# Where a chunked scan's matmuls are asked for: products with the inverse moved up to the chunk's first group, key and query products asked for in pairs

## The chip, the core and the metric

The kernel runs on one core of one Trainium2 chip. The metric is device time in microseconds (us) for one execution of the program; three executions were timed, and one more was taken with the hardware profiler. An execution holds one layer of an encoder for a sequence of 1024 tokens and 16 meta tokens, width 1024, everything in 32-bit floats.

## The reference, cut to what matters

The layer normalises its input, projects it with one wide matrix, and splits the result into streams. The stream that the change touches is the gated delta rule, for 8 heads of width 128, once forward and once backward over the sequence. Cut to what matters here, the reference does this for every head and direction:

```python
kk = jnp.einsum("bnhid,bnhjd->bnhij", k, k)                  # keys with keys, inside a chunk
lmat = jnp.where(strict, beta[..., :, None] * kk * decay, 0.0)
a = lmat + jnp.eye(CHUNK)
sol = lax.linalg.triangular_solve(a, rhs, lower=True, unit_diagonal=True)
qk = jnp.einsum("bnhid,bnhjd->bnhij", q, k) * decay          # queries with keys
...
def step(S, inp):                                            # one chunk
    v_new = u_c - jnp.einsum("bhcd,bhde->bhce", w_c, S)
    o_c = (jnp.einsum("bhcd,bhde->bhce", qd_c, S)
           + jnp.einsum("bhij,bhje->bhie", qk_c, v_new))
    S = S * gl_c[..., None, None] + jnp.einsum("bhcd,bhce->bhde", kd_c, v_new)
    return S, o_c
```

Around it stand a short convolution branch, gates, an output projection, a SwiGLU and a final normalisation. The change does not touch those.

## The kernel before, in words

The program has a first stage (the input projection with all eight heads' scans woven into it), and after it stages of large products alone. The change lies in the first stage.

**Dense work.** `dense_steps` (L328) makes the projection: a unit of 128 output columns takes three blocks of tokens (336, 320 and 384 wide, or two of 512), and each block is 24 matmuls into one PSUM bank: eight slices of the width times three terms (high part by high part, high by low, low by high), which together stand in for a full-precision product. The trace names them by their tiles, pm<-hTh,wh, pm<-al,wh and pm<-hTh,wl. There are 3744 of these matmuls in the stage.

**Streams.** Beside the dense units, generators bring the heads along: `g_decay` (masks of decay), `g_norm` (norms, and the products of keys with keys and queries), `g_inv` (the inverse of the triangular matrix), `g_scan` (the walk over chunks). They hand over at every `yield` with the time at which they want to go on. `run_streams` is called between any two dense matmuls and lets each stream that is due issue its next instructions; `pump` does the same for queues of VectorE work (convolutions, the inverse's substitution steps, norms).

**The planner's clock.** Nothing of this is known at run time: the order on each engine is written down once, by a planner that keeps an account T of how far TensorE ("pe"), VectorE ("dve") and ScalarE ("act") have got. `pe(ns)` adds to TensorE's account and returns its end plus 200 ns; `V(n, 1)` adds 130 + 1.042 n ns to VectorE's (263 ns for n = 128) and returns its end plus 370 ns. On the chip each engine then runs its own list in order and waits on semaphores, so where the account is wrong an engine waits, and everything behind the waiting instruction waits with it.

**A chunk of the scan** (`g_scan`, loop over i = 0..7). A head has 8 chunks of 128 tokens, and step i works on chunk i forward and chunk 7 - i backward, so most instructions come in twos. In order: keys by state into bank b1 (L853); queries by state into bank b2 (L856); VectorE makes r0 from b1 (L863); the inner products kept back from the chunk before, PQ by v2 (`late`, L892); the additions to the output (L834 and L839 on VectorE, squares at L843 on ScalarE); the inverse by r0 (L871, tiles pd<-r,NP), which is the step that the change moves; ScalarE scales its result to w and v2 (L878, L883); kn by w (L888); VectorE updates the state S (L902). In the first step of a head one direction has no state yet, so L853, L856 and L863 come once. At a head's end small VectorE instructions make a root (L920 to L499), eight instructions scale the output (L928), TensorE transposes it (L98) and ScalarE copies it out (L943).

**Keys by keys and queries** (`kkq`, L590, in `g_norm`). One matmul per chunk makes both products, 256 columns wide, into a bank of the three banks named pe. VectorE takes them off (L626 twice, L629 once) and the bank is free again; `freed_at` holds when, by the account. `ask` issues the next product once the bank it needs is free by that account.

**The border.** The last unit of dense work in this stage is a gate z; its VectorE step is L465 (tile rb) and its store is L467 (z_d<-rb). Behind it stands the next stage's first work: its own z products (L134 to L136), splits of weights (L179, wl<-raw,wh), and sums of the activations (L179, b<-hTh) in the space that rb used.

## Time and profile before

| | us |
|---|---|
| median of three timed runs | 1973.54 |
| lowest and highest of them | 1972.09, 1974.93 |
| the profiled execution's own time | 1973.36 |
| its span, first to last instruction | 1971.6 |

The profile page gives busy time by engine, a strip of 40 slices, and groups of instructions by source line. Its timeline gives the start and length of each instruction; rows that follow each other on one line are merged, with a count. A 32-bit product shows as two matmul records, so a pair of products reads x4. Lengths of matmuls overlap, since they are pipelined; what a matmul costs TensorE is read from start to start. PE is TensorE, PEld its weight loads, DVE VectorE, ACT ScalarE.

### The profile page before, as it was taken

To read this page: it belongs to the slowest core of one execution; us is meant where nothing else is said; L and a number is where in the kernel's file an instruction comes from. 1 tells how busy PE (TensorE), PEld (TensorE's weight loads), DVE (VectorE), ACT (ScalarE), POOL (GpSimd) and SP (SyncE) were. 2 spreads that over 40 slices of the span, in tenths; PEclk is the share of its full clock that TensorE was granted. 3 is DMA by queue.
4 is the path that set the end of the run, shared out by engine and by line. 5 is a ranking of instruction groups with operands and counts; after the bars stand their busy time and mean duration, and the time that the engine had idled before them with its cause. 6 is when DMAs were issued, how large, how long until landed. Compare 5 with 4: busy or idle time off the path is not lost.

```text
span 1971.6 us, 31923 instructions
## 1 busy us (share of the span) xinstructions
PE 1957.3 (99%) x11992; PEld 1719.6 (87%) x11992; DVE 1398.0 (71%) x3017; ACT 837.7 (42%) x1968; POOL 108.4 (5%) x410
## 2 busy tenths in 40 slices
PE   9999999999999999999999999999999999999998
PEld 8999999999999999888888888888888888878887
DVE  7888688888888888845954544468676765746575
ACT  6462364646464646343444211235333333324344
POOL 2011101010101010100000000000000000000000
PEclk9999999999999999999999999999999999999999
DMA  4122121212121212223246642133366654577654
GB/s 145 61 86 81 55 87 60 77 59 77 59 84 52 87 49 87 65 81 108 85 150 242 245 153 86 65 107 112 103 234 246 245 189 153 178 274 242 193 173 168
DMA packets 124704, 251.53 MB, mean 128 GB/s; under 512 B 44988, under 2 KB 46453, under 8 KB 122117
## 3 DMA queue, kind: packets, MB, share of 16 engines
q1 hardware_dynamic: 123957, 248.44, 37.8%
q8 instruction: 94, 1.54, 0.3%
q10 hardware_dynamic: 592, 1.05, 0.1%
q14 instruction: 61, 0.50, 0.1%
HBM read 181.20 MB, written 68.25 MB: 127 GB/s over the span
## 4 chain that ended last, share of the span: by engine, by line
PE 45%; DMA 3%; DVE 2%; ACT 1%; issue 0%; SPq 0%; DVEq 0%; ACTq 0%
PE pd L1446 12%; PE pe L1446 6%; PE pm L1446 4%; PE pe L2057 1%; PE pe L2055 1%; PE pe L2056 1%; PE pd L2057 1%; PE pd L2055 1%; PE pd L2056 1%; PE pe L134 1%; PE pe L135 1%; PE pd L135 1%; PE pd L134 1%; PE pe L136 1%; PE pd L136 1%; PE pm L2056 1%
## 5 line engine op out<-in xcount | busy, mean ns | idle before, releaser
L328 PE MATMUL pm<-hTh,wh 128*128 128x320 f32 (+4 forms) x1248 | 426.9, 347 | 0.3 <-ACT hTh L1096 0.2
L328 PE MATMUL pm<-hTh,wl 128*128 128x320 f32 (+4 forms) x1248 | 426.8, 347 | 0.0
L328 PE MATMUL pm<-al,wh 128*128 128x320 f32 (+4 forms) x1248 | 423.8, 345 | 0.0
L328 PEld LDWEIGHTS pm<-hTh,wh 128*128 128x128 f32 x1248 | 233.9, 188 | 10.7 <-ACT hTh L1096 0.9
L328 PEld LDWEIGHTS pm<-al,wh 128*128 128x128 f32 x1248 | 233.8, 188 | 10.7
L328 PEld LDWEIGHTS pm<-hTh,wl 128*128 128x128 f32 x1248 | 233.9, 188 | 10.2 <-POOL wl L1111 0.3
L102 DVE TENSOR_TENSOR al<-raw,ring_h 128x1024 fp32r<-128x1024 f32 x73 | 88.6, 1222 | 65.6 <-ACT ring_h L101 64.7
L101 ACT CAST ring_h<-raw 128x1024 fp32r<-128x1024 f32 x73 | 76.6, 1053 | 109.1 <-PE pe L2057 35.0
L982 DVE TENSOR_TENSOR wl<-raw,wh 128x512 fp32r<-128x512 f32 x112 | 75.3, 687 | 34.5 <-ACT wh L985 34.2
L350 DVE SCALAR_TENSOR_TENSOR kq<-ra,wc,kq 128x520 f32<-128x520 f32 x128 | 96.5, 754 | 3.5 <-ACT kq L380 2.0
L878 ACT ACTIVATE w<-pd,small 128x128 f32<-128x128 f32 x128 | 39.8, 362 | 123.4 <-PE pd L871 122.9
L483 DVE TENSOR_TENSOR tm<-fP,fN 128x135 f32<-128x135 f32 (+23 forms) x248 | 72.2, 291 | 4.8
L487 DVE TENSOR_TENSOR fP<-fP,tm 128x135 f32<-128x135 f32 (+23 forms) x248 | 71.9, 290 | 5.0
L985 ACT CAST wh<-raw 128x512 fp32r<-128x512 f32 x112 | 66.3, 624 | 3.8 <-issue 3.6
L101 ACT CAST wh<-raw 128x1024 fp32r<-128x1024 f32 x37 | 38.8, 1047 | 47.8 <-PE pe L135 10.4
L1994 ACT ACTIVATE b<-b 128x512 f32<-128x512 f32 x20 | 12.6, 632 | 101.6 <-DVE b L1412 101.6
L843 ACT ACTIVATE jk<-NP 128x128 f32<-128x128 f32 x64 | 19.9, 311 | 81.1 <-DVE NP L839 80.1
L102 DVE TENSOR_TENSOR wl<-raw,wh 128x1024 fp32r<-128x1024 f32 x37 | 45.1, 1219 | 10.2 <-ACT wh L101 10.0
L1446 PE MATMUL pd<-b_hl,wh 128*128 128x512 f32 x168 | 51.9, 390 | 0.0
L1412 DVE TENSOR_TENSOR b<-pd,b 128x512 f32<-128x512 f32 x21 | 14.5, 689 | 52.5 <-PE pd L1446 47.5
L350 DVE SCALAR_TENSOR_TENSOR vT<-ra,wc,vT 128x520 f32<-128x520 f32 x64 | 48.3, 754 | 1.4 <-ACT vT L380 0.7
L679 POOL TENSOR_TENSOR tm<-mP,mN 1x15 f32<-1x15 f32 (+7 forms) x120 | 36.9, 307 | 210.8 <-DMA mN<-ndm 202.4
(630 smaller groups left out, 4772.1 us busy)
## 6 DMA issues: line engine op xcount, KB each, us to landing
raw<-in_w_in_dram SPq DMA_DIRECT2D x72, 512.0 KB
raw<-in_w_gate_up_dram SPq DMA_DIRECT2D x44, 512.0 KB
sums<-in_w_down_dram SPq DMA_DIRECT2D x22, 512.0 KB
t_d<-sums SPq DMA_DIRECT2D x11, 1024.0 KB
raw<-s_d SPq DMA_DIRECT2D x44, 256.0 KB
raw<-t_d SPq DMA_DIRECT2D x44, 256.0 KB
act_d<-b SPq DMA_DIRECT2D x43, 256.0 KB
raw<-act_d SPq DMA_DIRECT2D x33, 256.0 KB
```

The lines of the kernel that those rows point to most:

```text
L101: nc.scalar.copy(hi, src)
L102: nc.vector.tensor_tensor(out=lo, in0=src, in1=hi.bitcast(F32), op=ALU.subtract)
L134: mm(po[:m, :n], wh[:, k, :m], xhk[:, t0:t0 + n], start=(k == 0), stop=False)
L328: mm(po[:, :n], ww[:, k], f(k)[:, t0:t0 + n], start=i == 0, stop=i == 3 * KT - 1)
L350: nc.vector.scalar_tensor_tensor(out=acc, in0=raw[:, h0 + t:h0 + t + hn], scalar=wc[:, t, col:col + 1], in1=acc, op0=ALU.mult, op1=ALU.add)
L483: nc.vector.tensor_tensor(out=tv, in0=fP[:, 0:r, j:j + 1].broadcast_to([P, r, n]), in1=fN[:, j:j + 1, j + 1:32].broadcast_to([P, r, n]), o ...
L487: nc.vector.tensor_tensor(out=fP[:, 0:r, j + 1:32], in0=fP[:, 0:r, j + 1:32], in1=tv, op=ALU.subtract)
L878: nc.scalar.activation(w[d], b2[:, 2 + d], AF.Copy, scale=ce[:, c, d:d + 1])
L982: nc.vector.tensor_tensor(out=u[1][1][:, k], in0=u[2][:, k], in1=u[1][0][:, k].bitcast(F32), op=ALU.subtract)
L985: nc.scalar.copy(u[1][0][:, k], u[2][:, k])
L1446: mm(po, x[:, k], at(y, k), start=i == 0 and not add_to, stop=i == 11, skip_group_check=add_to)
L2056: mm(bank[t], h_[:, c], l_[:, hi], start=False, stop=False)
```

## The change

In `ask`, the products of keys with keys and queries are issued two at a time, once the bank that the second of them needs is free by the account. In `g_scan`, the planner now counts VectorE's r0 as started at the end of the first pair (L853) and not of the second; the products of queries by state are written behind r0's instructions (they are L863 in the new file, and r0 is L859), and the products with the inverse (still L871) follow at once in the same group, without handing over, wherever by the account r0 will be there within 150 ns. Elsewhere the stream hands over as before.

```diff
--- before.py
+++ after.py
@@ -596,9 +596,9 @@
         def ask():
 
             nonlocal asked
-            while asked < NC and asked < len(freed_at) + 2 and freed_at[asked - 2] <= T["pe"]:
-                nxt.append(kkq(asked))
-                asked += 1
+            while asked < NC and asked - 1 < len(freed_at) and freed_at[asked - 1] <= T["pe"]:
+                nxt.extend((kkq(asked), kkq(asked + 1)))
+                asked += 2
         yield T["act"] + HOP
         nc.vector.tensor_scalar(out=ssk1, in0=ssk, scalar1=EPS, scalar2=None, op0=ALU.add)
         nc.vector.reciprocal(rk2, ssk1)
@@ -851,11 +851,7 @@
             b1, b2 = newbank(), newbank()
             for d in act_:
                 mm(b1[:, d], kT[:, cs(cd[d])], S[d], start=True, stop=True)
-            t = pe(215 * len(act_))
-            for d in act_:
-                mm(b2[:, d], qT[:, cs(cd[d])], S[d], start=True, stop=True)
             pe(215 * len(act_))
-            yield t
             r0 = [vS[:, cd[0]], vS[:, cd[1]]]
             for d in act_:
                 c = cd[d]
@@ -863,10 +859,14 @@
                 nc.vector.scalar_tensor_tensor(out=r0[d], in0=b1[:, d], scalar=negEG[:, c, hd[d]:hd[d] + 1], in1=vS[:, c],
                                                op0=ALU.mult, op1=ALU.add)
                 t = V(P, 1)
+            for d in act_:
+                mm(b2[:, d], qT[:, cs(cd[d])], S[d], start=True, stop=True)
+            pe(215 * len(act_))
             while late:
                 late.pop(0)()
             outputs()
-            yield t
+            if t > T["pe"] + 150:
+                yield t
             for d in range(2):
                 mm(b2[:, 2 + d], NP[:, cd[d], d], r0[d], start=True, stop=True)
             yield pe(430)
```

TensorE, early in the stage, head 0: the third and the fourth product of keys (L590) before, among dense matmuls (L328).

```order
L590 MATMUL pe_1489<-kq_308 128x256
L328 MATMUL pm_1452<-hTh,wh_1284 128x336
L328 MATMUL pm_1452<-al_126,wh_1284 128x336
L328 MATMUL pm_1452<-hTh,wl_1285 128x336
L328 MATMUL pm_1452<-hTh,wh_1284 128x336
L328 MATMUL pm_1452<-al_126,wh_1284 128x336
L328 MATMUL pm_1452<-hTh,wl_1285 128x336
L328 MATMUL pm_1510<-hTh,wh_1284 128x320
L328 MATMUL pm_1510<-al_124,wh_1284 128x320
L328 MATMUL pm_1510<-hTh,wl_1285 128x320
L590 MATMUL pe_1517<-kq_308 128x256
L328 MATMUL pm_1510<-hTh,wh_1284 128x320
```

The same place now:

```order
L328 MATMUL pm_1506<-al_124,wh_1284 128x320
L328 MATMUL pm_1506<-hTh,wl_1285 128x320
L590 MATMUL pe_1515<-kq_308 128x256
L590 MATMUL pe_1517<-kq_308 128x256
L328 MATMUL pm_1506<-hTh,wh_1284 128x320
L328 MATMUL pm_1506<-al_124,wh_1284 128x320
```

The third product no longer goes out ahead by itself; it waits for the fourth one's bank and both stand together.

TensorE, the last chunk of the last head, before: first pair, second pair, kept inner products, three dense matmuls, then the products with the inverse.

```order
L853 MATMUL pd_11993<-S_11979,kq_9477 128x128
L853 MATMUL pd_11993<-S_11981,kq_9477 128x128
L856 MATMUL pd_11994<-S_11979,kq_9477 128x128
L856 MATMUL pd_11994<-S_11981,kq_9477 128x128
L892 MATMUL pd_11932<-v_2028_11963,PQ_10011 128x128
L892 MATMUL pd_11932<-v_2029_11965,PQ_10011 128x128
L328 MATMUL pm_11974<-al_124,wh_11796 128x512
L328 MATMUL pm_11974<-hTh,wl_11797 128x512
L328 MATMUL pm_11974<-hTh,wh_11796 128x512
L871 MATMUL pd_11994<-r_2036_11999,NP_10480 128x128
L871 MATMUL pd_11994<-r_2037_12001,NP_10480 128x128
L328 MATMUL pm_11974<-al_125,wh_11796 128x512
```

And now:

```order
L853 MATMUL pd_12016<-S_12006,kq_9399 128x128
L853 MATMUL pd_12016<-S_12008,kq_9399 128x128
L863 MATMUL pd_12017<-S_12006,kq_9399 128x128
L863 MATMUL pd_12017<-S_12008,kq_9399 128x128
L892 MATMUL pd_11968<-v_2030_11992,PQ_10074 128x128
L892 MATMUL pd_11968<-v_2031_11994,PQ_10074 128x128
L871 MATMUL pd_12017<-r_2038_12020,NP_10323 128x128
L871 MATMUL pd_12017<-r_2039_12022,NP_10323 128x128
L328 MATMUL pm_12001<-hTh,wh_11701 128x512
```

The three dense matmuls that stood between the inner products and the inverse's are gone to other places; eight products of the scan stand in a row. In the whole program 18 of the 64 chunks are ordered like this (one of them with a dense matmul ahead of each L871); in the other 46 L871 still stands apart. The number of times that dense work is broken into falls from 358 to 331.

VectorE at the border, before: the root's last steps, the scaling of the output (L928), with the last two steps of gates z (L465) around it.

```order
L498 SCALAR_TENSOR_TENSOR small_10144<-small_10144 128x9
L499 SCALAR_TENSOR_TENSOR small_10144<-small_10144 128x9
L928 TENSOR_SCALAR NP_10480<-NP_10480,small_10144 128x128
L465 SCALAR_TENSOR_TENSOR rb_12045<-rb_12045,pm_11974 128x512
L928 TENSOR_SCALAR NP_10480<-NP_10480,small_10144 128x128 x7
L179 TENSOR_TENSOR wl_12148<-raw_12129,wh_12147 128x1024
L465 SCALAR_TENSOR_TENSOR rb_12095<-rb_12095,pm_12047 128x512
L179 TENSOR_TENSOR b_2054_12125<-hTh 128x2048
```

And now:

```order
L498 SCALAR_TENSOR_TENSOR small_10063<-small_10063 128x9
L179 TENSOR_TENSOR wl_12148<-raw_12129,wh_12147 128x1024
L465 SCALAR_TENSOR_TENSOR rb_12083<-rb_12083,pm_12001 128x512
L499 SCALAR_TENSOR_TENSOR small_10063<-small_10063 128x9
L497 TENSOR_TENSOR small_10063<-small_10063 128x9
L498 SCALAR_TENSOR_TENSOR small_10063<-small_10063 128x9
L499 SCALAR_TENSOR_TENSOR small_10063<-small_10063 128x9
L928 TENSOR_SCALAR NP_10323<-NP_10323,small_10063 128x128 x8
L179 TENSOR_TENSOR b_2054_12125<-hTh 128x2048
```

The last L465, whose store the next stage's L179 on b waits for, now stands ahead of the root's last four steps and of L928, and behind its first steps; L928 has become the last thing of the stage.

TensorE at the border, before: the last dense matmuls, then the eight transposes of the last head's output.

```order
L328 MATMUL pm_12047<-al_126,wh_11796 128x512
L328 MATMUL pm_12047<-hTh,wl_11797 128x512
L328 MATMUL pm_12047<-hTh,wh_11796 128x512
L328 MATMUL pm_12047<-al_126,wh_11796 128x512
L328 MATMUL pm_12047<-hTh,wl_11797 128x512
L98 MATMUL pd_12099<-ident,NP_10480 128x128 x4
L98 MATMUL pd_12106<-ident,NP_10480 128x128 x4
```

And now, 17 matmuls of the next stage's z (L134 to L136) later:

```order
L135 MATMUL pe_12150<-al_125,wh_12143 128x512
L136 MATMUL pe_12150<-hTh,wl_12144 128x512
L134 MATMUL pe_12150<-hTh,wh_12143 128x512
L98 MATMUL pd_12099<-ident,NP_10323 128x128 x3
L135 MATMUL pe_12150<-al_126,wh_12143 128x512
L98 MATMUL pd_12099<-ident,NP_10323 128x128
L98 MATMUL pd_12106<-ident,NP_10323 128x128 x2
L136 MATMUL pe_12150<-hTh,wl_12144 128x512
L98 MATMUL pd_12106<-ident,NP_10323 128x128 x2
L134 MATMUL pe_12150<-hTh,wh_12143 128x512
```

The transposes now stand among the next stage's products.

## Prediction, made before the changed kernel ran

> **What bounds the kernel now.** I read the page first, then who TensorE waited for, then the stretches of the first stage.
>
> ```profile
> span 1971.6 us, 31923 instructions
> PE 1957.3 (99%) x11992; PEld 1719.6 (87%) x11992; DVE 1398.0 (71%) x3017; ACT 837.7 (42%) x1968; POOL 108.4 (5%) x410
> ```
>
> ```profile
> PE pd L98 <- POOL ident masks.py:199: 1.5, 1, 1.5
> PE pe L1446 <- ACT b L1989: 1.2, 1, 1.2
> PE pe L590 <- DVE PQ L629: 1.1, 2, 0.8
> PE pe L98 <- DVE xr L1082: 0.9, 1, 0.9
> PE pm L2056 <- DVE al L102: 0.8, 1, 0.8
> PE pd L98 <- DVE ss L162: 0.7, 1, 0.7
> PE pm L328 <- ACT hTh L1096: 0.2, 1, 0.2
> ```
>
> ```profile
> 300.00:500.00 200.00, 200.00 (x1711) 192.26 (x1710) 172.29 (x505) 103.67 (x343) 23.84 (x94) 1.00 0.23 70
> 500.00:700.00 200.00, 200.00 (x1707) 191.54 (x1706) 173.72 (x519) 104.81 (x347) 23.26 (x94) 1.00 0.23 68
> 700.00:923.00 223.00, 222.85 (x1753) 201.07 (x1752) 159.00 (x497) 102.98 (x331) 21.28 (x79) 1.00 0.23 73
> ```
>
> The first numbers behind each stretch are its length and TensorE's busy time; they are equal, with the granted clock at 1.00. In the whole span TensorE waited 1.5 + 1.2 + 1.1 + 0.9 + 0.8 + 0.7 + 0.2 = 6.4 us for others, and of these the change can reach one row: L590 behind L629, 1.1 us in two places. So TensorE bounds the stage, and what counts is what its matmuls cost from start to start and whether it newly waits. That the scan's chain becomes shorter is worth nothing by itself.
>
> A row of busy time does not prove that the array has no room. [...]
>
> **The change part by part.** First, what does a group cost? The last chunk of the last head:
>
> ```profile
> 911.42 0.40 PE L328 MATMUL pm<-hTh,wh 128*128 128x512 f32 x1
> 911.66 0.61 PE L853 MATMUL pd<-S,kq 128*128 128x128 f32 x4
> 912.10 0.61 PE L856 MATMUL pd<-S,kq 128*128 128x128 f32 x4
> 912.31 0.61 DVE L863 SCALAR_TENSOR_TENSOR r<-pd,negEG,vS 128x128 f32<-128x128 f32 x2 [0.47 <-PE pd L853]
> 912.55 0.61 PE L892 MATMUL pd<-v,PQ 128*128 128x128 f32 x4
> 912.92 0.48 PE L328 MATMUL pm<-al,wh 128*128 128x512 f32 x1
> 913.24 0.39 PE L328 MATMUL pm<-hTh,wl 128*128 128x512 f32 x1
> 913.46 0.40 PE L328 MATMUL pm<-hTh,wh 128*128 128x512 f32 x1
> 913.70 0.61 PE L871 MATMUL pd<-r,NP 128*128 128x128 f32 x4
> 914.06 0.47 PE L328 MATMUL pm<-al,wh 128*128 128x512 f32 x1
> 914.37 0.39 PE L328 MATMUL pm<-hTh,wl 128*128 128x512 f32 x1
> ```
>
> A dense matmul of 512 takes 0.23 us to the next start (913.24 to 913.46, 913.46 to 913.70 a little more). The one right behind a group takes 0.31 or 0.32, which looks like a fee of 0.08 for each group. But it is the tail of the last small product: the group of six takes 913.24 - 911.66 - 0.23 = 1.35 us, or 0.225 a product, and the group of two takes 914.37 - 913.70 - 0.23 = 0.44, or 0.22 a product. Twos, fours and sixes cost the same for each product. Eight in a row come to 8 x 0.222 = 1.78 against 1.35 + 0.44 = 1.79: **0.01 us for each of the 18 chunks, 0.2 us in all**.
>
> The same for the keys, one product and then two:
>
> ```profile
> 124.83 0.59 PE L590 MATMUL pe<-kq 128*128 128x256 f32 x2
> 125.07 0.53 PE L328 MATMUL pm<-hTh,wh 128*128 128x384 f32 x1
> 125.44 0.33 PE L328 MATMUL pm<-al,wh 128*128 128x384 f32 x1
> 125.61 0.33 PE L328 MATMUL pm<-hTh,wl 128*128 128x384 f32 x1
> 142.84 1.03 PE L590 MATMUL pe<-kq 128*128 128x256 f32 x4
> 143.51 0.59 PE L328 MATMUL pm<-hTh,wl 128*128 128x512 f32 x1
> 143.94 0.40 PE L328 MATMUL pm<-hTh,wh 128*128 128x512 f32 x1
> ```
>
> One costs 125.44 - 124.83 - 0.17 (a dense matmul of 384) = 0.44 us, two cost 143.94 - 142.84 - 0.23 = 0.87. Two singles are 0.88. With 64 such products the pairs save 0.01 x 32 or 0.3 us at the very most; I count 0.1. What the pairs can take away is the wait for L629: between 0 and the 1.1 us of its row. The first of a pair now uses a bank that has been free for longer, and the second comes 0.435 us behind it (half of 0.87), which is cover for a bank that VectorE frees a little late. I take 0.6 off, near the middle since neither end has a better row.
>
> Next, what the 18 new places of L871 can cost. Nothing dense stands between L892 and L871 any more, so if r0 is late, TensorE stands still and all dense work stands behind it. In the rows above, VectorE was free: r0 began 0.65 us after L853 began (912.31 - 911.66) and both were done 0.61 later, at 1.26. In a row of eight, the first L871 has its turn at 6 x 0.222 = 1.33 and needs the first r0, and the second at 1.55 and needs the second: it is there 0.3 us early. Where VectorE is busy it looks like this:
>
> ```profile
> 418.60 0.74 PE L853 MATMUL pd<-S,kq 128*128 128x128 f32 x4
> 419.80 0.60 DVE L863 SCALAR_TENSOR_TENSOR r<-pd,negEG,vS 128x128 f32<-128x128 f32 x2
> ```
>
> Here r0 began at 1.20 and ended at 1.80, which would hold the second L871 up by 1.80 - 1.55 = 0.25 us. The bounds are thus 0 and 18 x 0.25 = 4.5 us. The change chooses its places by the planner's account: t is VectorE's start plus 2 x 263 + 370 = 896 ns, and TensorE stands at 2 x 430 = 860 ns past the end of the first pair, so t is under 860 + 150 only where VectorE is at most 114 ns behind at that end. That picks the cases of the first kind. I take 0.2 us for all 18, for a few in which the account is off, and keep 4.5 as the far end.
>
> In the other 46 chunks L871 is asked for up to 0.43 us sooner than before. In the rows above it came at 913.70, 0.78 us after r0's end at 912.92, so this uses up slack and adds no wait; cost 0, or the same 0.25 each where the account is badly off. ScalarE's steps behind L871 and the S update behind them keep their distance to it.
>
> Last, the border. What is moved there is VectorE's list, and with it the store of the last gate:
>
> ```profile
> 916.46 0.60 PE L892 MATMUL pd<-v,PQ 128*128 128x128 f32 x4
> 921.40 0.29 DVE L928 TENSOR_SCALAR NP<-NP,small 128x128 f32<-128x128 f32 x1
> 922.21 1.46 DVE L928 TENSOR_SCALAR NP<-NP,small 128x128 f32<-128x128 f32 x7
> 923.05 1.04 PE L98 MATMUL pd<-ident,NP 128*128 128x128 f32 x8
> 924.10 1.22 DVE L179 TENSOR_TENSOR wl<-raw,wh 128x1024 fp32r<-128x1024 f32 x1 [0.44 <-ACT wh L1497]
> 925.24 0.68 DVE L465 SCALAR_TENSOR_TENSOR rb<-rb,pm 128x512 f32<-128x512 f32 x1
> 931.15 2.29 DVE L179 TENSOR_TENSOR b<-hTh 128x2048 f32<-128x2048 f32 x1 [5.23 <-DMA z_d<-rb]
> ```
>
> Before, 27 dense matmuls stood between the last inner products and the end of the dense work at 923.05; now 10 do, so L892 is at about 923.05 - 10 x 0.23 - 0.45 = 920.3. L928 began 921.40 - 916.46 = 4.94 us after it. Now L179 and L465 also stand ahead of it, from 924.10 to 925.24 and on to 925.92 less 0.08 of overlap, 1.7 us: L928 begins at about 920.3 + 4.94 + 1.7 = 926.9 and its eight end near 928.7 (1.46 us for seven makes 0.21 each). TensorE comes to the first L98 after 17 matmuls of the next stage, at 923.05 + 17 x 0.23 = 927.0, and would be through eight transposes and the two matmuls between them by 928.3; its last one waits until about 928.8. That is a new wait of **0.7 us** (0 to 1.5, as the estimate of L928 shifts). Behind it, VectorE's long sums (L179 on b) do not start when VectorE is free, but when the store of the last gate has landed, 5.23 us after VectorE had stopped. L465 moves by about 0.2 to 0.4 us, so these sums do too; I count that as covered by TensorE's own 0.7.
>
> The sum against the profiled execution: -0.2 - 0.1 - 0.6 + 0.2 + 0.7 = 0.0 us on its 1973.36 us (span 1971.6 and 1.76 around it). The median of the runs is 0.18 above it, so the forecast for a median is **1973.5 us**.
>
> **The rivals.** *A group does have a fee.* Then the 0.08 us behind each group is real and 27 fewer groups (358 to 331) save 27 x 0.08 = 2.2 us: 1971.3. For it speaks the row of 0.31 behind each group, against it the equal cost of a product in twos and sixes. Chance 0.10. [...]
>
> *VectorE is late where the planner believes it free.* L871 in its new place then holds up TensorE, the engine that bounds the stage: 18 x 0.25 = 4.5 us, 1978. It decides where r0's second half ends later than 1.55 us after L853's start. For it: the row at 419.80. Against it: VectorE's account is kept op by op, and at 912.31 VectorE sat idle for 0.47 us waiting for L853. Chance 0.07.
>
> *The border passes its delay on.* If the last L465 slips by the whole tail of the root and not by 0.4, the sums on b, and what TensorE takes from them, slip too; I price it at the eight L928, from 926.9 to 928.7: another 1.8 us, 1975.3. Against it stands the order: L465 is ahead of L928. Chance 0.12.
>
> **How the numbers follow.** Forecast 0.69, fee 0.10, late VectorE 0.07, border 0.12, and 0.02 for something that gives TensorE more than all of its visible waits. A measurement of this kernel can tell about 0.2%, 3.9 us, from no change. The forecast, the fee and the border are within it: 0.91. Late VectorE is the slower side, 0.07; faster is 0.02. The range goes from the fee's 1971.3, a little lower for the run-to-run spread of the times before, to past the border's 1975.3: 1971.0 to 1976.2. It leaves out late VectorE and the far ends, about 1 in 10.
>
> **What would show each step.** In the new profile, eight products in a row at 1.78 us and pairs of L590 at 0.87 confirm that there is no fee; rows of eight shorter than 1.7 refute it. A row of waits with L871 behind L859 shows late VectorE, with its sum. The row of L590 behind L629 should be gone or under 0.5 us. A wait of L98 behind L928 near 927 us, and the start of L179 on b near 931.4, test the border. The prediction is wrong if TensorE's waits in the first stage differ from before by more than some 2 us.

## The result, and the profile after

The changed kernel takes 1987.57 us (median of six runs, 1983.48 to 1991.55) against 1974.94 us for the kernel before on the same chip (six runs, 1972.09 to 1976.74). The ratio is 1.0064 with a 95% interval of 1.005 to 1.0079: it is **12.6 us slower**. I had forecast no difference, 1973.5 us.

The two profiled executions lie 15.1 us apart (1988.45 and 1973.36 us). The page after, its span and its busy time by engine:

```profile
span 1986.7 us, 31921 instructions
PE 1964.1 (99%) x11992; PEld 1720.2 (87%) x11992; DVE 1398.1 (70%) x3017; ACT 838.4 (42%) x1968; POOL 109.5 (6%) x410
```

The counts of each engine's instructions are the same as before. The last dense matmul (L328) of the first stage starts at 937.15 us where it started at 922.82, so 14.3 of the 15.1 us arise in that stage. Whom TensorE waited for in the kernel after (total us, number of times, longest):

```profile
PE pd L853 <- DVE S L902: 2.3, 6, 0.7
PE pe L590 <- DVE PQ L629: 1.9, 2, 1.4
PE pd L1446 <- DVE b L1412: 1.9, 1, 1.9
PE pd L738 <- issue: 1.8, 1, 1.8
PE pe L98 <- DVE xr L1082: 1.8, 1, 1.8
PE pd L98 <- POOL ident masks.py:199: 1.5, 1, 1.5
PE pm L328 <- DVE wl L982: 0.9, 1, 0.9
...
PE pd L98 <- DVE NP L928: 0.6, 2, 0.4
...
PE pd L759 <- DVE XT L751: 0.4, 1, 0.4
PE pd L806 <- DVE wide L804: 0.3, 1, 0.3
```

The row of L871, where I looked for a late VectorE, is not there. New in the stage are the rows of L853, L738, L328 behind L982, L928, L759 and L806, and L590 has grown from 1.1 us. Each is small, and they lie in different places. The grown row of L98 behind L1082 (0.9 us before) lies ahead of the stage's first dense matmul, which starts at the same time as before (13.47 us, 13.51 before); the new row of L1446 behind L1412 lies behind the stage, at 1517.30 us.

This list knows only idle time that the profiler could name. I therefore sorted the stage in a second way, from the start of its first dense matmul to the start of its last. Each TensorE instruction takes the time from its predecessor's start to its own; from it goes the median that the same neighbourhood (line and width of the predecessor and of the one before, line of the instruction) has in the nineteen kernels of the table below, and the rest is put down to the instruction that came late. "At the scan" below sums this for the products of a chunk (L853, L856, L871, L888, L892 by their text), "elsewhere" is all other lines. Kernels are to be compared, the absolute value means little. For the kernel before it gives 0.3 us at the scan and 5.8 elsewhere, for the changed one 6.2 and 14.1: **+5.9 at the scan, +8.3 elsewhere**. The medians themselves sum to 0.2 us more. Together 14.4 us, the stage's whole loss.

**The scan's share.** One of the six places, in the changed kernel's timeline (start, length, engine, operation, idle time before it in brackets):

```profile
723.58 0.60 PE L888 MATMUL pd<-w,kn 128*128 128x128 f32 x4
...
723.72 1.17 ACT L985 CAST wh<-raw 128x512 fp32r<-128x512 f32 x2
...
724.40 0.69 DVE L982 TENSOR_TENSOR wl<-raw,wh 128x512 fp32r<-128x512 f32 x1 [1.88 <-ACT wh L985]
...
726.32 0.59 DVE L902 SCALAR_TENSOR_TENSOR S<-S,eGl,pd 128x128 f32<-128x128 f32 x2
...
726.71 0.75 PE L853 MATMUL pd<-S,kq 128*128 128x128 f32 x4 [0.73 <-DVE S L902]
```

The chunk was done early on TensorE (L888 at 723.58). But VectorE stood for 1.88 us at a step of a weight split (L982) whose cast (L985) ScalarE only began at 723.72, and four small steps followed that (725.01 to 726.32) before the state's update L902 had its turn. TensorE then came to the next chunk's L853 0.73 us too early. In the other five places VectorE idles less, or not at all; L902 simply stands behind its queue (steps L350, L358, L483, L487, L982). The chunk ahead of the wait shown is one of the 18 with a row of eight; in four of the six places it is one in which L871 stands apart.

**Elsewhere.** Three stalls make up the most of it. First, a readback: the inverse's data go out by the stores L689, come back by the loads L694, and VectorE takes them at L713. The last head's, before and after:

```profile
840.19 1.66 SPq L689 DMA_DIRECT2D pd<-fP  x3
...
849.11 1.93 SPq L694 DMA_DIRECT2D NP<-pd  x4
...
851.56 0.43 DVE L713 STREAM_TRANSPOSE XT<-NP 32x256 f32<-32x256 f32 x1 [2.49 <-DMA NP<-pd]
```

```profile
862.45 1.66 SPq L689 DMA_DIRECT2D pd<-fP  x3
...
870.57 3.31 SPq L694 DMA_DIRECT2D NP<-pd  x4
...
876.23 0.43 DVE L713 STREAM_TRANSPOSE XT<-NP 32x256 f32<-32x256 f32 x1 [10.55 <-DMA NP<-pd]
...
880.10 1.29 DVE L982 TENSOR_TENSOR wl<-raw,wh 128x512 fp32r<-128x512 f32 x2
...
880.85 0.50 PE L328 MATMUL pm<-hTh,wl 128*128 128x512 f32 x1 [0.89 <-DVE wl L982]
```

The way from L689 to L713 took 11.4 us before (851.56 - 840.19) and 13.8 after. But VectorE now reached L713 when only some 3 us of it had gone by, at 876.23 - 10.55 = 865.7, since in the new list less of its work stands ahead of it; it stood for 10.55 us where it had stood for 2.49. The weight split L982 is queued behind it, and TensorE waits 0.89 us for that. A smaller case, 2.95 us, comes shortly before the longest wait of L590, at the second product of a pair:

```profile
692.97 0.43 DVE L713 STREAM_TRANSPOSE XT<-NP 32x256 f32<-32x256 f32 x1 [2.95 <-DMA NP<-pd]
...
695.03 0.42 DVE L629 TENSOR_TENSOR PQ<-pe,PQ 128x256 f32<-128x256 f32 x1
...
695.61 0.67 PE L590 MATMUL pe<-kq 128*128 128x256 f32 x2 [1.40 <-DVE PQ L629]
```

Second, TensorE stopped in a burst of 32 by 32 products, 1.80 us for which the profile names no engine ("issue"), and third, its granted clock was 0.50 right behind that:

```profile
592.61 0.24 PE L738 MATMUL pd<-NP,T 32*32 32x32 f32 x4
594.65 0.18 PE L738 MATMUL pd<-NP,T 32*32 32x32 f32 x1 [1.80 <-issue]
...
597.81 0.63 PE L328 MATMUL pm<-hTh,wh 128*128 128x512 f32 x1
598.24 0.63 PE L328 MATMUL pm<-al,wh 128*128 128x512 f32 x1
```

Dense matmuls of 512 columns are 0.43 us apart there, where 0.23 is usual. The stretch of the stop and the one behind it (length, TensorE's busy time, granted clock):

```profile
592.00:595.90 3.90, 2.10 (x102) 1.00 0.06 19
595.92:599.31 3.39, 3.39 (x10) 0.50 0.02 5
```

At half clock for 3.4 us, TensorE loses an estimated 1.7 us (0.50 x 3.4). The stop costs 1.8 us and the wait for L982 0.9; with the L590 row's growth of 0.8 these are 5.2 of the 8.3 us elsewhere. The rest is scattered in pieces of some tenths.

### The profile page after: what moved, and what is told of

It reads as the page before. It is cut to its first block, busy times and chain, and to the rows that moved or that the text cites. A ratio compares the mean times of both kernels' runs of the same rounds, so it can differ in the third digit from the quotient of the medians.

```text
span 1986.7 us, 31921 instructions
## 1 busy us (share of the span) xinstructions
PE 1964.1 (99%) x11992; PEld 1720.2 (87%) x11992; DVE 1398.1 (70%) x3017; ACT 838.4 (42%) x1968; POOL 109.5 (6%) x410
## 3 DMA queue, kind: packets, MB, share of 16 engines
q8 instruction: 94, 1.54, 0.3%
## 4 chain that ended last, share of the span: by engine, by line
PE 52%; DMA 3%; DVE 2%; issue 0%; SPq 0%; ACT 0%; DVEq 0%; ACTq 0%
PE pd L1446 13%; PE pe L1446 6%; PE pm L1446 4%; PE pm L328 2%; PE pe L135 1%; PE pe L134 1%; PE pe L136 1%; PE pe L2056 1%; PE pe L2055 1%; PE pe L2057 1%; PE pd L2056 1%; PE pd L2055 1%; PE pd L2057 1%; PE pd L134 1%; PE pd L135 1%; PE pd L136 1%
## 5 line engine op out<-in xcount | busy, mean ns | idle before, releaser
L328 PE MATMUL pm<-al,wh 128*128 128x320 f32 (+4 forms) x1248 | 426.1, 347 | 0.0
L328 PE MATMUL pm<-hTh,wh 128*128 128x320 f32 (+4 forms) x1248 | 424.9, 346 | 0.3 <-ACT hTh L1096 0.2
L328 PE MATMUL pm<-hTh,wl 128*128 128x320 f32 (+4 forms) x1248 | 423.9, 345 | 0.9 <-DVE wl L982 0.9
L328 PEld LDWEIGHTS pm<-hTh,wl 128*128 128x128 f32 x1248 | 234.1, 189 | 11.7 <-DVE wl L982 1.3
L328 PEld LDWEIGHTS pm<-hTh,wh 128*128 128x128 f32 x1248 | 234.1, 189 | 11.3 <-ACT hTh L1096 0.9
L328 PEld LDWEIGHTS pm<-al,wh 128*128 128x128 f32 x1248 | 234.1, 189 | 10.3
L982 DVE TENSOR_TENSOR wl<-raw,wh 128x512 fp32r<-128x512 f32 x112 | 76.5, 689 | 33.4 <-ACT wh L985 33.0
L350 DVE SCALAR_TENSOR_TENSOR kq<-ra,wc,kq 128x520 f32<-128x520 f32 x128 | 96.9, 757 | 1.2 <-DVE kq L350 0.5
L483 DVE TENSOR_TENSOR tm<-fP,fN 128x135 f32<-128x135 f32 (+23 forms) x248 | 72.5, 292 | 4.5 <-DMA fN<-nd 1.0
L487 DVE TENSOR_TENSOR fP<-fP,tm 128x135 f32<-128x135 f32 (+23 forms) x248 | 72.1, 291 | 4.8
L985 ACT CAST wh<-raw 128x512 fp32r<-128x512 f32 x112 | 66.8, 627 | 3.7 <-issue 3.6
L1994 ACT ACTIVATE b<-b 128x512 f32<-128x512 f32 x20 | 12.6, 631 | 104.8 <-DVE b L1412 104.8
L1412 DVE TENSOR_TENSOR b<-pd,b 128x512 f32<-128x512 f32 x21 | 14.5, 689 | 53.8 <-PE pd L1446 53.8
L533 ACT ACTIVATE PQ<-PQ,negG 128x128 f32<-128x128 f32 x128 | 43.1, 394 | 21.3 <-DVE PQ L528 21.2
L1446 PE MATMUL pd<-b_hl,wh 128*128 128x512 f32 x168 | 51.9, 390 | 0.0
L350 DVE SCALAR_TENSOR_TENSOR vT<-ra,wc,vT 128x520 f32<-128x520 f32 x64 | 48.4, 756 | 2.5 <-ACT vT L380 1.3
```

Of the source, the lines that this page charges most:

```text
L328: mm(po[:, :n], ww[:, k], f(k)[:, t0:t0 + n], start=i == 0, stop=i == 3 * KT - 1)
L350: nc.vector.scalar_tensor_tensor(out=acc, in0=raw[:, h0 + t:h0 + t + hn], scalar=wc[:, t, col:col + 1], in1=acc, op0=ALU.mult, op1=ALU.add)
L483: nc.vector.tensor_tensor(out=tv, in0=fP[:, 0:r, j:j + 1].broadcast_to([P, r, n]), in1=fN[:, j:j + 1, j + 1:32].broadcast_to([P, r, n]), o ...
L487: nc.vector.tensor_tensor(out=fP[:, 0:r, j + 1:32], in0=fP[:, 0:r, j + 1:32], in1=tv, op=ALU.subtract)
L533: nc.scalar.activation(PQ[:, c, d], PQ[:, c, d], AF.Exp, bias=negG2[:, c, hd:hd + 1])
L982: nc.vector.tensor_tensor(out=u[1][1][:, k], in0=u[2][:, k], in1=u[1][0][:, k].bitcast(F32), op=ALU.subtract)
```

## The experiments

My theory when I began (A) was that the change's visible parts are right in the forecast, but that a re-ordered plan meets waits that the planner's account does not hold, wherever they are. The rivals: the early booking of r0 makes the state's updates late (B); TensorE is held at L871 (C, the one priced in the prediction); the pairs of keys cost it (D). The account's entries that the edits change are: ARRIVE, the delay in ns after which a mask's load is taken to be there, and LAND, that after which a store is taken to have landed, so that its data can be read back; `pe(435)`, the booking of one product L590.

### All runs

Each line is against the kernel before on the same chip: difference of medians, ratio's 95% interval, chunks in rows of eight, then the two sums of the second sorting for the profiled execution, which is one execution of each kernel.

| kernel | us | against before | 95% interval | rows of eight | at the scan | elsewhere |
|---|---|---|---|---|---|---|
| before | | 0 | | 0 | 0.3 | 5.8 |
| e15_replan_arrive2 | 1973.93 | -0.3 | 0.9991 to 1.0009 | 0 | 1.1 | 4.9 |
| e8_replan_land | 1974.45 | +0.2 | 0.9991 to 1.001 | 0 | 0.7 | 7.6 |
| e4_replan_arrive | 1976.93 | +3.4 | 1.0005 to 1.0024 | 0 | 1.9 | 6.2 |
| e16_replan_land2 | 1978.49 | +4.3 | 1.0015 to 1.0034 | 0 | 1.7 | 11.2 |
| e7_replan_kkq | 1979.3 | +5.0 | 1.0015 to 1.0034 | 0 | 0.7 | 11.7 |
| e1_keys_alone | 1979.39 | +5.9 | 1.0018 to 1.0037 | 0 | 0.7 | 10.6 |
| e3_scan_no_merge | 1977.0 | +3.5 | 1.0004 to 1.0024 | 0 | 2.9 | 6.7 |
| e18_scan_slack | 1976.9 | +3.5 | 1.0007 to 1.0026 | 0 | 2.4 | 7.3 |
| e11_after_no_merge | 1979.33 | +6.1 | 1.0021 to 1.0047 | 0 | 4.1 | 7.0 |
| e2_scan_alone | 1980.63 | +7.1 | 1.0022 to 1.0046 | 17 | 7.0 | 7.2 |
| e9_after_land | 1979.06 | +5.8 | 1.0023 to 1.0044 | 16 | 5.7 | 7.5 |
| e10_after_kkq | 1980.9 | +7.6 | 1.0025 to 1.0055 | 16 | 4.2 | 8.3 |
| the change | 1987.57 | +12.6 | 1.005 to 1.0079 | 18 | 6.2 | 14.1 |
| e12_scan_booked | 1979.58 | +6.3 | 1.0022 to 1.0048 | 30 | 4.2 | 9.3 |
| e5_after_booked | 1980.42 | +6.2 | 1.0015 to 1.0041 | 35 | 4.7 | 10.2 |
| e13_booked_land | 1981.45 | +7.3 | 1.0023 to 1.0053 | 38 | 7.8 | 6.6 |
| e14_booked_kkq | 1983.74 | +9.6 | 1.0031 to 1.0064 | 37 | 7.1 | 7.8 |
| e17_after_gap | 1980.05 | +6.7 | 1.0019 to 1.0046 | 19 | 2.8 | 10.3 |

(e6_after_split, +55.4 us, is left out here; it loses in another way, told below.)

### The two parts apart

e1_keys_alone is the kernel before with the pairs of keys:

```diff
-            while asked < NC and asked < len(freed_at) + 2 and freed_at[asked - 2] <= T["pe"]:
-                nxt.append(kkq(asked))
-                asked += 1
+            while asked < NC and asked - 1 < len(freed_at) and freed_at[asked - 1] <= T["pe"]:
+                nxt.extend((kkq(asked), kkq(asked + 1)))
+                asked += 2
```

> The kernel before with only the key and query products asked for in twos. If the loss of 12.6 us lies in holding TensorE at the inverse's products (theory C) or in booking VectorE's r0 too early (theory B), this one is within 1 us of before. If any re-ordering of the plan costs, because waits arise between engines that the planner's account does not hold (theory A), it is 2 to 10 us slower than before. If the pairs themselves are at fault (theory D), it carries most of the 12.6 us and its waits stand at L590.

e2_scan_alone is the kernel before with the rest of the change; e3_scan_no_merge is that with the hand-over always made:

```diff
-            if t > T["pe"] + 150:
-                yield t
+            yield t
```

> The kernel before with only the change to the scan (r0 booked from the end of the first pair, 17 merged groups). Theories B and C: 10 to 13 us slower than before. Theory A: some 2 to 12 us slower, and not the rest of what the keys alone leave. Theory D: within 1 us of before.

> The scan's change with the early booking of r0, but the stream always hands over before the inverse's products, so that none stands in the first group. Theory C: within 1 us of before. Theory B: 8 to 13 us slower, as the booking is the same. Theory A: slower by some 2 to 12 us, with waits in other places than in the changed kernel.

Measured: +5.9 us for the keys, +7.1 for the scan's part, +3.5 for it without merging. The first two add up to 13.0, about the whole. In e2 the seventeen rows of eight take 1.782 to 1.796 us, median 1.79, so merging holds nobody up in the row itself: theory C falls for this kernel, and for the change, whose merged rows lose 0.15 us at L871 by the second sorting. (In the four kernels below that merge 30 to 38 chunks, they lose 0.9 to 2.2 us there.) The groups of six that are left take 1.475 us in the mean in e2 and 1.450 in the change, where all take 1.353 before: 39 x 0.12 = 4.8 us, nearly all of it waiting for S. The keys' loss is another thing. TensorE's waits in e1, the first row:

```profile
PE pd L98 <- DVE NP L746: 2.3, 1, 2.3
```

One wait of transposes for a step of an inverse, which ends at 286.31 us and is no product of keys; the row of L590 has gone from the list.

### What any new plan costs

Five kernels have nothing changed but one figure of the planner's account, so that it writes the same program in another order: e4_replan_arrive, e7_replan_kkq, e8_replan_land, and later e15_replan_arrive2 and e16_replan_land2.

```diff
-    ARRIVE = 10000
+    ARRIVE = 10400
```

```diff
-            return pk, pe(435)
+            return pk, pe(445)
```

```diff
-    LAND = 5500
+    LAND = 5700
```

```diff
-    ARRIVE = 10000
+    ARRIVE = 9600
```

```diff
-    LAND = 5500
+    LAND = 5300
```

> The kernel before, with none of the change: one constant of the planner's account (how long a mask's load takes to arrive) is 10400 ns in place of 10000. The same instructions on each engine, in an order that differs in a hundred places on TensorE. Theory A: 2 to 10 us slower than before. Theories B, C and D: within 1.5 us of before.

> The kernel before with none of the change: a product of keys is booked at 445 ns in place of 435, the smallest shift of the plan that was tried (about a third as many rows stand elsewhere as in the other re-plan). Theory A: 0 to 6 us slower than before. Theories B, C and D: within 1.5 us of before.

> The kernel before with none of the change: a store's landing is booked at 5700 ns in place of 5500. Theory A: 1 to 8 us slower than before. Theories B, C and D: within 1.5 us of before.

> The kernel before with ARRIVE at 9600 ns where 10000 stood; nothing else. Scatter of plans: +0 to +5 us, as the three neutral plans so far (+3.4, +5.0, +0.2), by waits in other places. If the plan of the kernel before is in no way singled out, there should be plans below it as well: -3 to +3 us.

> The kernel before with LAND at 5300 ns where 5500 stood; nothing else. Scatter of plans: +0 to +5 us. If the plan of the kernel before is not singled out: -3 to +3 us.

Measured: +3.4, +5.0, +0.2, -0.3 and +4.3 us. Theory A is shown as far as it goes: a plan alone moves the time by up to 5 us. The dearest of them has the keys' wait as its first row:

```profile
PE pd L98 <- DVE NP L746: 2.5, 1, 2.5
```

e16 has it too (2.3 us). So e1's +5.9 lies hardly above what neutral plans give, by the same wait, and theory D has no run that bears it out. The kernel before is at the low end of its six plans, whose mean is 2.1 us above it.

Is the change's 12.6 us then such an accident as well? e9_after_land and e10_after_kkq are neutral plans of the changed kernel:

```diff
-    LAND = 5500
+    LAND = 5700
```

```diff
-            return pk, pe(435)
+            return pk, pe(445)
```

> The whole change, with the planner's LAND at 5700 ns where 5500 stood; nothing else. This only makes another plan of the changed kernel. Theory A (most of the loss comes with the plan that happened to come out, since each plan meets other waits): the loss moves by several us, to anywhere from +4 to +16 us against the kernel before. Rival (the loss belongs to the change itself, above all to the early booking of r0): it stays at +11 to +14.5 us.

> The whole change, with a product of keys with keys and queries booked at 445 ns where 435 stood; nothing else. A second neutral plan of the changed kernel. Theory A: +4 to +16 us, and not where the first one is. Rival (a property of the change): +11 to +14.5 us, as the changed kernel itself.

Measured: +5.8 and +7.6 us. About half of the 12.6 us is an accident of the one plan: "elsewhere" falls from 14.1 to 7.5 and 8.3 us, which is within what plans of the kernel before have (4.9 to 11.7). But "at the scan" stays, 5.7 and 4.2 us. By their medians all three plans of the changed kernel lie above all six plans of the kernel before, though the nearest two, e9 at +5.8 and e7 at +5.0 us, overlap in their intervals. At the scan the two sets are clear of each other: 4.2 to 6.2 against 0.3 to 1.9 us. Theory A alone does not carry that.

### Booking r0 where it starts

Theory B says that the account takes r0 to start with the end of the pair, while in the rows it starts later. In the quoted row of the prediction r0 began 0.65 us after L853 began, which is 0.215 after the pair's 0.43. e5_after_booked books that, with the bound for merging moved by the same amount; e12_scan_booked does so without the keys; e13_booked_land and e14_booked_kkq are e5 with the two neutral edits of e9 and e10.

```diff
             r0 = [vS[:, cd[0]], vS[:, cd[1]]]
+            T["dve"] = max(T["dve"], T["pe"] + 215)
...
-            if t > T["pe"] + 150:
+            if t > T["pe"] + 365:
```

> The changed kernel, but VectorE's r0 is booked from 215 ns behind the end of the first pair, which is where the trace of before shows it to start (0.645 us behind the first start, not 0.43), and the bound for merging is raised by the same 215 ns; 35 chunks merge in place of 18. Theory B (the early booking makes the account run ahead of VectorE): most of the loss of 12.6 us goes, to under 4 us slower than before. Theory A (any re-ordered plan meets waits that the account does not hold): still 3 to 12 us slower than before, with waits at other places. If merging itself held TensorE up (theory C), it would be slower than the changed kernel by 5 us or more.

> The scan's part alone, with r0 booked where VectorE really begins it, 215 ns behind the end of the pair, and merged by the same rule. Theory B (the early booking makes the S updates late): the waits of L853 behind S are gone, the groups that are not merged go back to some 1.39 us, and the time is +0 to +4 us against the kernel before, where the scan's part with the early booking was +7.1. Rival (the order of writing, queries by state behind r0, costs by itself): +6 to +8 us still.

> The changed kernel with r0 booked right, and LAND at 5700 ns. If what was left (+6.2 us) is the scatter of plans, this plan lands somewhere else, in the spread that plans of the kernel before have: 0 to +5 us, with no row of L853 behind S over 0.5 us. If it is a property of the change, +5.5 to +7 us again.

> The changed kernel with r0 booked right, and a product of keys booked at 445 ns. Scatter of plans: 0 to +5 us, and not where the one with LAND at 5700 is. Property of the change: +5.5 to +7 us again.

Measured: +6.2, +6.3, +7.3 and +9.6 us. e5 looked like a success for B, since half of the loss was gone and with it the row of L853 behind S, though B had asked for less than 4 us. It was the plan: with the early booking other plans lose no more (e9, e10), and with the right one e13 and e14 lose up to 9.6. In e5 the lateness has only moved, from L853 (4.6 to 1.1 us by the second sorting) to L872, which waits for r0 (0.9 to 2.3), and to L889, which waits for w (0.6 to 1.2). **B falls** as the cause of the size. e12's own rival is not ruled out: its +6.3 us lies where the new order of writing (queries by state behind r0, with one hand-over less) was to cost +6 to +8 by itself, and no kernel has that order alone.

e11_after_no_merge is the whole change, but always handing over (the edit of e3):

> Both parts of the change, but the products with the inverse never follow at once: the stream always hands over, as in the kernel before. r0 is still booked from the end of the first pair, and keys are still asked for in twos. If the two parts add up, 5.9 us (keys alone) and 3.5 us (the scan's part without merging) make +9.4 us. Theory A: it is again one plan among others, +2 to +9 us. Rival (the merging carries the loss): about +6 us, what the keys cost alone. Rival (the early booking carries it, with or without merging): +11 us or more, and the waits of L853 behind S are there as in the changed kernel.

Measured: +6.1 us, with 4.1 us at the scan. That time is what the rival of the merging gave it, but the scan's waits are still there. Without merging the scan's share is 2.9 (e3) and 4.1, with it 4.2 to 7.8 in eight kernels, against 0.3 to 1.9 in the plans of the kernel before. So the early asking has a part; that merging adds to it is likely but not shown, as the two ranges all but touch.

### Giving the slack back

What is common to all these kernels is that a chunk's steps follow each other sooner. If that is what TensorE pays for at the scan, time given back should take the waits away. e17_after_gap is the whole change, with the next chunk asked for 400 ns later; e18_scan_slack is e3 with 300 ns ahead of the inverse's products.

```diff
             for d in range(2):
                 output(b2, cd[d], d, d in act_)
-            yield t
+            yield t + 400
```

```diff
             outputs()
-            yield t
+            yield t + 300
             for d in range(2):
                 mm(b2[:, 2 + d], NP[:, cd[d], d], r0[d], start=True, stop=True)
```

> The whole change, with each chunk's first products asked for 400 ns later. Theory (the change takes out slack that had covered late S updates): the waits at the scan's own products fall from about 6 us in the changed kernel to under 3, L853 behind S most of all; the time lands at +2 to +8 us, by what the new plan meets elsewhere. Rival (these waits come from the merged rows and what they do to VectorE and ScalarE, not from the start of the next chunk): 4 to 7 us of them stay, and the time is +6 us or more.

> The scan's part alone, without merging, and the products with the inverse asked for 300 ns later. Theory (slack): the waits at the scan's products, 2.9 us in this kernel without the 300 ns, fall to what the kernel before and its neutral plans have, 0.2 to 1.8 us; the time lands at +0 to +5 us. Rival: 2.5 to 4 us of them stay.

In e17 the waits at the scan fall from 6.2 to 2.8 us, and those of L853 from 4.6 to 0.1. All of TensorE's waits in e17, by the same list as for the change:

```profile
PE pe L98 <- DVE xr L1082: 2.4, 1, 2.4
PE pd L1446 <- DVE b L1412: 2.0, 1, 2.0
PE pd L738 <- issue: 1.9, 3, 1.0
PE pd L98 <- POOL ident masks.py:199: 1.5, 1, 1.5
PE pd L98 <- DVE NP L746: 1.2, 1, 1.2
PE pd L98 <- DVE ss L162: 0.7, 1, 0.7
PE pm L328 <- ACT vT L380: 0.6, 1, 0.6
PE pm L328 <- ACT hTh L1096: 0.2, 1, 0.2
PE pd L871 <- DVE r L859: 0.2, 1, 0.2
```

L853 is gone from it; the groups of six are back at 1.352 us in the mean. There are still 19 rows of eight, so the lateness of S goes with the slack at the chunk's start and not with the merged row. L871 now loses 1.7 us where it lost 0.9. The time, +6.7 us, shows what the new plan meets elsewhere instead (10.3 us: L738 behind issue 1.9, L98 behind L746 1.2). Against the neutral plans of the change (+5.8 and +7.6) it is no gain, so the 3.4 us that left the scan are seen in the sorting and not in a time.

e18 came out half as expected: L870 (the inverse's products there) no longer waits, its groups go from 0.477 to 0.446 us, but the waits for S hardly move (2.6 to 2.3 us), and the time is the same +3.5. Its sum at the scan, 2.4 us, stays above the 0.2 to 1.8 us that the theory asked for. In these two kernels slack helped at the step ahead of which it was given.

### One that did worse

The rows at 724.40 suggest to move the weight split out of S's way. e6_after_split books L982 behind ScalarE's cast:

```diff
-            V(512)
+            on("dve", 130 + 1.042 * 512, T["act"] + HOP)
```

> The changed kernel, but the planner books the low half of a weight split on VectorE (L982) only when the cast on ScalarE that it needs (L985) is done by the account. Theory A in its narrow form (the state update L902 is late because it stands behind a low half that waits for its cast): TensorE's waits at L853 for S fall from 2.3 us by the wait list, and about 4.5 us by start to start, to under 1 us, and the time falls by 3 us or more below the changed kernel's. Theory B: no gain, within 2 us of the changed kernel.

Measured: 2029.65 us, +55.4 (1.0266 to 1.0296). The account now holds VectorE busy where it waits, every job of VectorE is put later, and the dense work runs out (at 890.0 us) before the scans do. From then on TensorE has nothing between their steps. The 100 us behind 900, by engine (after the length the busy time of TensorE, its weight loads, VectorE, ScalarE and GpSimd, then the granted clock):

```profile
900.00:1000.00 100.00, 66.23 (x553) 55.92 (x551) 56.75 (x191) 31.57 (x112) 0.00 (x0) 0.76 0.09 27
```

TensorE idles for a third of them, and its clock is 0.76 in the mean. This says nothing on whether L982 ahead of S is dear; that stays untested.

## Why the prediction was wrong, step by step

**No fee for a group: right.** The last chunk's row of eight in the changed kernel:

```profile
925.89 0.61 PE L853 MATMUL pd<-S,kq 128*128 128x128 f32 x4
926.33 0.61 PE L863 MATMUL pd<-S,kq 128*128 128x128 f32 x4
926.53 0.61 DVE L859 SCALAR_TENSOR_TENSOR r<-pd,negEG,vS 128x128 f32<-128x128 f32 x2 [0.47 <-PE pd L853]
926.78 0.61 PE L892 MATMUL pd<-v,PQ 128*128 128x128 f32 x4
927.22 0.61 PE L871 MATMUL pd<-r,NP 128*128 128x128 f32 x4
...
927.59 0.48 PE L328 MATMUL pm<-hTh,wl 128*128 128x512 f32 x1
927.91 0.39 PE L328 MATMUL pm<-hTh,wh 128*128 128x512 f32 x1
```

927.91 - 925.89 - 0.23 = 1.79 us, as worked out; most pairs of L590 take 0.86 or 0.87. A product of the scan costs 0.22 to 0.225 us in the quoted groups of two, six and eight alike (1.79 / 8 = 0.224), so the 27 fewer breaks of the dense work have nothing to save.

**Eighteen new places of L871, 0.2 us: right in mechanism and size.** The list has no row of L871; by the second sorting L871 lost 0.15 us in the rows of eight, and 0.74 in the other chunks. The late-VectorE rival was right that VectorE is late where the account has it free, and wrong about the place where TensorE pays for it.

**Pairs of keys, -0.6 us: wrong in sign.** The row of L590 grew from 1.1 to 1.9 us, through one wait of 1.4 behind a late readback. In e1 the pairs' own effect has the sign that I gave it: by the second sorting L590 loses 0.5 us less than before.

**The border, +0.7 us: right.** In the changed kernel, 14 us later than drawn:

```profile
941.22 1.66 DVE L928 TENSOR_SCALAR NP<-NP,small 128x128 f32<-128x128 f32 x8
941.57 0.72 PE L98 MATMUL pd<-ident,NP 128*128 128x128 f32 x3 [0.17 <-DVE NP L928]
...
945.12 2.29 DVE L179 TENSOR_TENSOR b<-hTh 128x2048 f32<-128x2048 f32 x1 [2.24 <-DMA z_d<-rb]
```

TensorE waits 0.6 us in two places for L928, and L179 on b starts 8.0 us behind the last dense matmul, where it was 8.3 (931.15 - 922.82).

**The other 46 chunks: this is the step that failed.** I wrote that L871, asked for up to 0.43 us sooner, "uses up slack and adds no wait", and that ScalarE's steps and the S update "keep their distance to it". They keep it on an engine that is free. VectorE, at 71 to 87% of the stretches that the prediction shows, takes its list in order (at 724.40 L982 had stood 1.88 us for its cast, and L902, behind it in the list, began at 726.32), so L902 moves up only in part with L888; the next chunk's L853 does move, since the planner places it by an account in which L902 did. The two profiles show it, from first start to first start in the mean of the 56 steps from one chunk to the next. L871 starts 1.59 us behind L853 where it was 2.01. But L902 starts 1.43 us behind L888 where it was 1.28 (1.24 to 1.37 in the six plans of the kernel before, 1.36 to 1.53 in the six kernels with the early booking and no slack given back), and the next L853 follows 2.29 us behind L888, hardly later than the 2.22 before. So the time between the end of an L902 and the L853 that reads its state (the closer of the two directions) falls: it is under 0.1 us in 2 of the 56 steps before and in 9 after (1 to 5 in the six plans of the kernel before, 7 to 13 in those six kernels).

What I called slack was what covered VectorE's lateness, and I had put its price at 0. The scan's products lost 4.2 to 7.8 us in the plans with merging and 0.3 to 1.9 in the plans of the kernel before; in the change most of it is L853 behind S, 4.6 us, of which 3.0 follow a chunk with L871 apart and 1.6 a row of eight. So the 18 places, priced at L871 alone, pass lateness on as well. e17 supports the mechanism: with 400 ns given back, that time is under 0.1 us in 1 step of 56, and the waits of L853 are gone. That the whole loss at the scan would come off the time is not shown.

**The step that was not there.** The sum held only what happens at the places that the change names. But the edits re-order the whole list of every engine from the first pair of keys on, and five neutral plans show that this alone is worth -0.3 to +5.0 us here. In the change's own plan it was worth 8.3 us elsewhere. None of my rivals was a plan that meets other waits; the range of 5.2 us in all had no room for it.

What stays open: why plans of the kernel before meet fewer waits than others. Three of six, the kernel before among them, lie within 0.5 us, the others at +3.4 to +5.0, and I have no mechanism for it. Whether the new order of writing around r0 costs something by itself has no run of its own. How much of the scan's share is merging (4.2 to 7.8 us with it, 2.9 and 4.1 without) and how much early asking rests on single profiles of each kernel. Whether the split L982 can be kept away from S without putting all of VectorE's work later was not tried beyond e6. No version beat the kernel before.

## What to carry to other kernels

Where an order is planned ahead from an account, price a change of the plan by neutral plans first: nudge a figure that means nothing, and take the scatter as the floor of your range. Slack ahead of a step on the engine that bounds the kernel need not be waste; here it was the cover for an in-order engine that is late by the account, and shortening a chain that was not the bound spent that cover. When the loss shows up as many short waits in unrelated places, sort the start-to-start times by line against several kernels before believing one row.

## What the runs showed of the hardware

In the changed kernel TensorE stopped for 1.80 us with no engine named for it (the row at 594.65, "issue"). In this stop a transfer of the queue that the page calls instruction ran from 592.46 to 593.42 us, by the trace's record of its packets; the page counts 94 of them:

```profile
q8 instruction: 94, 1.54, 0.3%
```

1.54 MB in 94 packets are 16 KB each. The stop came in a burst of 32 by 32 products, of which 78 had started within the 0.7 us before it, and it ended 1.23 us behind the end of the transfer (594.65 - 593.42); 58 such transfers start in the 937 us up to the end of this stage, one every 16 us. Shorter stops in such bursts (L738 or L741 behind "issue", 0.2 to 1.3 us each) are in twelve of the other kernels. That TensorE waited for its instructions there is not shown: the profile names nothing for the stop, and no run here took the transfers away.

Behind this stop the granted clock was 0.50, for 3.413 us by its record (from 595.91 us). TensorE had been busy for 2.10 of the 3.90 us before (the row 592.00:595.90), and for 1.61 of the last 3.41 (592.50 to 595.91). The changed kernel has another record of 0.50, of the same length, behind the stage, at 1517.51 us, beside the wait of 1.9 us for L1412; TensorE had been busy for 1.49 of the 3.41 us before it. The kernel before has none before its last 2 us, though near its end TensorE was busy for no more than 1.48 us from 1963.03 to 1966.45: up to 1969.80 the clock was still 1.00. So these traces do not show what made the clock fall.

The granted clock also differs between executions of one kernel: of the changed kernel's six, the two at a mean of 0.999 took 1983.48 and 1984.37 us, the two at 0.997 took 1988.45 and 1991.55.
